# Putting the recurrence's 64x64 products on all four array tiles

## The chip, the cores and the metric

The kernel runs on one core of a Trainium2 chip. A core has a matrix engine (PE, which multiplies a moving operand by a stationary one and writes to the accumulation memory PSUM), three engines for element-wise work (DVE, ACT, POOL) and a queue engine (SP), which mostly issues transfers here. Memory on the core has 128 partitions; PSUM has eight banks. The metric is the device time of one execution in microseconds, the median of several runs. Lower is better.

The PE array is 128 rows by 128 columns. A product with 64 rows of stationary operand and 64 columns of output uses one of four tiles: rows 0-63 or 64-127 (the partitions on which the operands lie) by columns 0-63 or 64-127 (the partitions of PSUM to which the result goes). "Straight" tiles write to the partitions that they read from, "crossed" tiles write to the other half.

## The reference

One layer of a hybrid decoder for a prompt of 256 positions and 8 single-position decode sequences, width 2048: a gated feed-forward network of width 5504, then a mixing stage (an input projection, windowed attention with 16 query heads, and a linear recurrence with 16 heads of 64x64 state), an output projection, a second feed-forward network, and a final normalisation. All in float32. The part that matters is the recurrence, per head:

```
sa = S @ (-kk_t)
S  = S * exp(lw_t)[None, :] + outer(sa, kk_t * a_t) + outer(v_t, k_t)
y_t = S @ r_t
```

## The kernel before, in words

The kernel keeps activations transposed: features on partitions, 256 + 8 = 264 positions along the free dimension. Weights stream from memory in 128x512 chunks (`chunk`, L121): SP loads one, ACT rounds it to a "hi" part (L128), DVE makes the rest "lo" (L59 through L129), and PE does three products of 264 moving columns for each 128x128 block (`gemm`, L132). These weight products are named acc<-s,hi and the like in the profile. There are 1288 chunks and four hi and four lo buffers.

In the mixing stage the heads come in eight pairs, the two heads of a pair on the two halves of the partitions, and the pairs in four batches of two. The prompt's 256 positions are cut into four chunks of 64. For each pair `prep` (L415) makes the factors of the chunk form: Gm (products of keys and values of positions, masked), BT, KR and UV, and the products `gv` (L517) and, for the decode sequences, `dps` (L523). For each batch `chain` (L542) inverts a triangular matrix for each head and chunk (X, Y, TT on DVE, then the 32x32 products at L584 and L595), and then does the following, all with 64x64 blocks:

- W/U (L608): one product with 128 moving columns gives W and U of a head and chunk, the two heads on the two straight tiles. W goes to the tile `W` (L611), U to the free half of the tile `uv` (L615).
- P/G (L623, L626): W times BT gives P, copied to `PT` (L629); W times a part of Gm is added to KR (L630).
- N and Y (L637, L643): products with 128 rows and 64 columns over `uv`.
- three steps (L649 to L666), one for each later chunk: P times the state S (into `ps`), S times KR added to Y (into `pY`), and two DVE operations per pair that give the next S.
- Y is copied out of PSUM (L668), normalised (`gnorm`, L696) and gated.

`prep` and `chain` are generators: at a `yield` they hand over to the next weight product group, so that small products stand between weight products in PE's order. The order within each engine's queue is not that of the source: a scheduler orders the instructions of the whole program by a timeline of its own, with priorities. Each engine then runs its queue strictly in that order. The output projection's first part waits for batches 0 and 1 (L919), its second for batches 2 and 3.

PSUM banks for small products are taken by `mp` (L118) from a ring of five; weight products use a ring of three (L115). A bank is 128 partitions by 512 float32.

## Time and profile before

| | us |
|---|---|
| time, median of 3 runs | 1982.49 (1981.63 to 1985.6) |
| span of the profiled execution, first to last instruction | 1978.1 |
| PE busy | 1962.6 |
| DVE busy | 1318.0 |
| ACT busy | 1037.1 |
| POOL busy | 267.2 |

The profiled execution has only its span recorded; a time of its own is not among the listed runs, which lie 3.5 to 7.5 us above that span. The mixing stage lies between about 780 and 1160 us, the small products of `chain` between about 885 and 1090 us. In the profile a 32-bit product appears as two records (two passes), and "busy" counts the whole latency of overlapping records, so the pace of a stage is read from the start of one group to the start of the next. A released wait is shown in square brackets behind an instruction.

### The profile page before, as it was taken

The numbers are of one execution on the slowest core, as the hardware profiler recorded it, in microseconds if no ns is written. First come the engines' busy times: TensorE is split into PE (matmuls) and PEld (weight loads), VectorE is DVE, ScalarE is ACT, GpSimd is POOL, SyncE is SP. The second block draws the span as 40 slices with busy tenths as digits, with TensorE's granted clock in tenths as the row PEclk, the third lists the DMA queues.
The fourth block names the chain that finished last, engine by engine and source line by source line (L and its number), as shares of the span: only waits on it lengthen the run. The fifth ranks groups of instructions, "written<-read, shape, count | busy, mean of one in ns | idle before, by whom it ended". The sixth has DMA issues, their size and how long they took to land.

```text
span 1978.1 us, 45244 instructions
## 1 busy us (share of the span) xinstructions
PE 1962.6 (99%) x17011; PEld 1944.7 (98%) x17011; DVE 1318.0 (67%) x2591; ACT 1037.1 (52%) x2069; POOL 267.2 (14%) x382
## 2 busy tenths in 40 slices
PE   9999999999999999999999999999999999999998
PEld 9999999999999999999999999999999999999998
DVE  5865555655556567799988766866666666666655
ACT  5644444444444456666656754654444444444445
POOL 0401001010010113222211000210101001010012
PEclk9999999999999999999999999999999999999999
DMA  7565565655555567554545455565666566666654
GB/s 238 178 191 191 184 191 193 183 185 174 188 180 182 182 189 230 162 165 147 147 140 172 134 161 180 177 182 187 189 185 194 182 192 188 190 192 181 192 179 147
DMA packets 218875, 357.26 MB, mean 181 GB/s; under 512 B 33552, under 2 KB 72352, under 8 KB 218656
## 3 DMA queue, kind: packets, MB, share of 16 engines
q1 hardware_dynamic: 212144, 345.76, 56.1%
q10 hardware_dynamic: 6512, 8.61, 1.3%
q8 instruction: 133, 2.18, 0.4%
q14 instruction: 86, 0.70, 0.1%
HBM read 346.67 MB, written 9.69 MB: 180 GB/s over the span
## 4 chain that ended last, share of the span: by engine, by line
PE 96%; DVE 2%; DMA 1%; issue 1%; ACT 1%; SPq 0%; DVEq 0%; ACTq 0%
PE acc L75 88%; PE m L75 8%; DVE lo L59 0%; ACT t L69 0%; DMA x<-in_x 0%; DMA raw<-in_wout 0%; DVE y L59 0%; DVE st L59 0%; DVE Xt L59 0%; DMA sa<-gm 0%; DMA ld<-in_sT 0%; ACT hi L128 0%; PE m L505 0%; DVE t L705 0%; DVE gm L59 0%
## 5 line engine op out<-in xcount | busy, mean ns | idle before, releaser
L59 DVE TENSOR_TENSOR lo<-raw,hi 128x512 fp32r<-128x512 f32 (+1 forms) x1288 | 869.6, 679 | 526.9 <-ACT hi L128 504.5
L128 ACT CAST hi<-raw 128x512 fp32r<-128x512 f32 (+1 forms) x1288 | 777.4, 607 | 839.5 <-PE acc L75 766.0
L75 PE MATMUL acc<-s,hi 128*128 128x264 f32 x5940 | 1110.9, 286 | 2.3 <-DVE o L62 1.0
L75 PEld LDWEIGHTS acc<-s,hi 128*128 128x128 f32 x5940 | 923.4, 188 | 6.7 <-ACT hi L128 1.8
L75 PE MATMUL acc<-s,lo 128*128 128x264 f32 x2970 | 847.5, 286 | 0.5 <-DVE lo L59 0.5
L75 PEld LDWEIGHTS acc<-s,lo 128*128 128x128 f32 x2970 | 558.7, 188 | 2.2 <-DVE lo L59 0.9
L75 PE MATMUL acc<-t,hi 128*128 128x264 f32 x2752 | 502.8, 284 | 0.0
L75 PEld LDWEIGHTS acc<-t,hi 128*128 128x128 f32 x2752 | 426.0, 188 | 0.0
L75 PE MATMUL acc<-t,lo 128*128 128x264 f32 x1376 | 388.5, 284 | 0.0
L59 POOL TENSOR_TENSOR t<-t,t 128x264 f32<-128x264 f32 (+1 forms) x148 | 151.0, 1020 | 1146.6 <-ACT hi L128 789.4
L75 PEld LDWEIGHTS acc<-t,lo 128*128 128x128 f32 x1376 | 258.1, 188 | 0.0
L75 PE MATMUL acc<-y,hi 128*128 128x264 f32 x648 | 123.7, 284 | 0.0
L75 PEld LDWEIGHTS acc<-y,hi 128*128 128x128 f32 x648 | 101.2, 188 | 0.1
L75 PE MATMUL acc<-y,lo 128*128 128x264 f32 x324 | 91.9, 284 | 0.0
L59 DVE TENSOR_TENSOR t<-acc,t 128x264 f32<-128x264 f32 x156 | 67.4, 432 | 35.8 <-PE acc L75 35.5
L59 POOL TENSOR_TENSOR o<-o,o 128x264 f32<-128x264 f32 x43 | 35.8, 833 | 235.8 <-ACT o L69 231.8
L75 PE MATMUL acc<-o,hi 128*128 128x264 f32 x324 | 62.4, 282 | 0.0
L75 PEld LDWEIGHTS acc<-y,lo 128*128 128x128 f32 x324 | 60.8, 188 | 0.0
L69 ACT ACTIVATE t<-t 128x264 f32<-128x264 f32 (+1 forms) x110 | 46.6, 424 | 8.8 <-DVE t L433 5.5
L62 DVE SCALAR_TENSOR_TENSOR s<-acc,s 128x264 f32<-128x264 f32 x96 | 40.6, 427 | 15.5 <-PE acc L75 15.1
L75 PEld LDWEIGHTS acc<-o,hi 128*128 128x128 f32 x324 | 49.9, 188 | 0.0
L75 PE MATMUL m<-s,hi 128*128 128x264 f32 x260 | 47.9, 284 | 0.0
(261 smaller groups left out, 1283.5 us busy)
## 6 DMA issues: line engine op xcount, KB each, us to landing
raw<-in_gu SPq DMA_DIRECT2D x688, 256.0 KB, 3.3
raw<-in_dn SPq DMA_DIRECT2D x224, 256.0 KB, 2.8
raw<-in_win SPq DMA_DIRECT2D x152, 256.0 KB, 3.4
raw<-in_dn SPq DMA_DIRECT2D x160, 192.0 KB, 2.7
raw<-in_wout SPq DMA_DIRECT2D x64, 256.0 KB, 3.2
xsp<-x ACTq DMA_DIRECT2D x16, 132.0 KB, 3.4
s<-xsp SPq DMA_DIRECT2D x16, 132.0 KB, 4.0
ld<-in_sT SPq DMA_DIRECT2D x16, 128.0 KB, 2.9
```

The lines of the kernel that those rows point to most:

```text
L59: return e.tensor_tensor(out=out, in0=a, in1=b, op=op)
L62: return V.scalar_tensor_tensor(out=out, in0=a, scalar=s, in1=b, op0=op0, op1=op1)
L69: return A.activation(out=out, in_=in_, func=f, **k)
L75: return TE.matmul(out, lhsT, rhs, start=start, stop=stop, **k)
L128: A.copy(hi[:, :w], raw[:, :w])
```

## The change

Products that used only the two straight tiles are distributed over four:

- W and U are separate products of 64 columns. U goes to the crossed tiles, so head h's U lies in PSUM on the other half's partitions, and W stays on the straight tiles. W of chunk 0, which nobody reads, is no longer computed. U and W have a bank each for both pairs of the batch, instead of one bank per pair. The copies into `uv` read from the other half, one for each half instead of one for each half and pair.
- P goes to the crossed tiles and G to the straight ones, in a bank each; the copies into `PT` swap the halves.
- In the three steps the products for `ps` stay straight, those for `pY` go crossed, and the two kinds alternate. The first products for `pY` also write to the other half. The copy out of `pY` is split in halves, one on ACT and one on DVE.
- In `prep` the products for `gv` (crossed already) and `dps` (straight already) alternate instead of following one another, with both banks taken at the start.

```diff
-                gv = mp()
-                for c in range(4):
+                gv, dps = mp(), mp()
+                for i in range(NB):
+                    c, g = i // 2, i % 2
                     for h in range(2):
                         r, o = HALF[h], HALF[1 - h]
-                        mm(gv[r, c * 64:c * 64 + 64], bt.Gm[k][h][o, c, 0:64], bt.UV[o, c, k, r])
+                        mm(dps[r, 2 * i:2 * i + 2], st[i // 4][r, i % 4, :], XD[r, 6:8, p, i])
+                        if h == g:
+                            mm(gv[r, c * 64:c * 64 + 64], bt.Gm[k][h][o, c, 0:64], bt.UV[o, c, k, r])
                 A.copy(KR[:, 2], gv[:, :256].rearrange("p (c t) -> p c t", c=4))
-                dps = mp()
-                for i in range(NB):
-                    for h in range(2):
-                        r = HALF[h]
-                        mm(dps[r, 2 * i:2 * i + 2], st[i // 4][r, i % 4, :], XD[r, 6:8, p, i])
...
-                wus = [mp() for _ in range(n)]
+                ub, wb = mp(), mp()
                 for k in range(n):
                     for c in range(4):
+                        x = (k * 4 + c) * 64
                         for h in range(2):
-                            r = HALF[h]
-                            mm(wus[k][r, c * P:c * P + P], TT[r, k * 4 + c, :], bt.KR[k][r, 0:3:2, c, :])
+                            r, o = HALF[h], HALF[1 - h]
+                            mm(ub[o, x:x + 64], TT[r, k * 4 + c, :], bt.KR[k][r, 2, c, :])
+                            if c:
+                                mm(wb[r, x:x + 64], TT[r, k * 4 + c, :], bt.KR[k][r, 0, c, :])
+                v = wb[:, :n * 256].rearrange("p (k c t) -> p k c t", k=n, c=4)
                 for k in range(n):
-                    v = wus[k].rearrange("p (c t) -> p c t", c=4)
-                    (A.copy, V.tensor_copy)[k % 2](W[:, k], v[:, 1:4, 0:64])
-                for k in range(n):
-                    v = wus[k].rearrange("p (c t) -> p c t", c=4)
-                    for h in range(2):
-                        (V.tensor_copy, A.copy)[h](uv[HALF[h], :, k, HALF[h]], v[HALF[h], :, 64:128])
+                    (A.copy, V.tensor_copy)[k % 2](W[:, k], v[:, k, 1:4, :])
+                v = ub[:, :n * 256].rearrange("p (k c t) -> p c k t", k=n, c=4)
+                for h in range(2):
+                    (V.tensor_copy, A.copy)[h](uv[HALF[h], :, :, HALF[h]], v[HALF[1 - h]])
                 yield
-                pbs = [mp() for _ in range(n)]
+                pb, gb = mp(), mp()
                 for k in range(n):
                     for c in range(1, 4):
...
-                            mm(pbs[k][r, x:x + 64], W[r, k, c - 1, :], bt.BT[k][r, c, r])
...
-                            mm(pbs[k][r, x + 64:x + P], W[r, k, c - 1, :], bt.Gm[k][h][r, c, 64:128])
+                            mm(pb[o, x:x + 64], W[r, k, c - 1, :], bt.BT[k][r, c, r])
+                            mm(gb[r, x:x + 64], W[r, k, c - 1, :], bt.Gm[k][h][r, c, 64:128])
+                v = pb[:, :n * 192].rearrange("p (k c t) -> p k c t", k=n, c=3)
+                for h in range(2):
+                    A.copy(PT[HALF[h]], v[HALF[1 - h]])
...
-                            mm(pY[r, x:x + 64], uv[:, c, k, r], bt.Gm[k][h][:, c, 64:128],
+                            mm(pY[HALF[1 - h], x:x + 64], uv[:, c, k, HALF[h]], bt.Gm[k][h][:, c, 64:128],
                                k + c == 0, c == 0, skip_group_check=True)
...
                         for h in range(2):
-                            r = HALF[h]
+                            r, o = HALF[h], HALF[1 - h]
                             mm(ps[r, k * 64:k * 64 + 64], PT[r, k, c - 1, :], S[r, k])
-                    for k in range(n):
-                        for h in range(2):
-                            r = HALF[h]
-                            x = (k * 4 + c) * 64
-                            mm(pY[r, x:x + 64], S[r, k], bt.KR[k][r, 1, c, :], False, True, skip_group_check=True)
+                            mm(pY[o, x:x + 64], S[r, k], bt.KR[k][r, 1, c, :], False, True, skip_group_check=True)
...
                 for k in range(n):
-                    A.copy(Ys[k][:, :NP], pY[:, k * NP:(k + 1) * NP])
+                    for h in range(2):
+                        (A.copy, V.tensor_copy)[h](Ys[k][HALF[h], :NP], pY[HALF[1 - h], k * NP:(k + 1) * NP])
```

More of the change, by code (lines that the diff above doesn't have):

```diff
@@ L627, in chain @@
+                v = pb[:, :n * 192].rearrange("p (k c t) -> p k c t", k=n, c=3)
+                for h in range(2):
+                    A.copy(PT[HALF[h]], v[HALF[1 - h]])
+                v = gb[:, :n * 192].rearrange("p (k c t) -> p k c t", k=n, c=3)
                 for k in range(n):
-                    v = pbs[k][:, :384].rearrange("p (c t) -> p c t", c=3)
-                    A.copy(PT[:, k], v[:, :, 0:64])
-                    tt(V, bt.KR[k][:, 1, 1:4, :], v[:, :, 64:128], bt.KR[k][:, 1, 1:4, :], ALU.add)
+                    tt(V, bt.KR[k][:, 1, 1:4, :], v[:, k], bt.KR[k][:, 1, 1:4, :], ALU.add)
@@ L651, in chain @@
                     for k in range(n):
+                        x = (k * 4 + c) * 64
                         for h in range(2):
[L653 removed]
+                            r, o = HALF[h], HALF[1 - h]
                             mm(ps[r, k * 64:k * 64 + 64], PT[r, k, c - 1, :], S[r, k])
[L655 to L659 removed]
+                            mm(pY[o, x:x + 64], S[r, k], bt.KR[k][r, 1, c, :], False, True, skip_group_check=True)
                     Z, Sn = ring((P, n, 64), "Z", 2), ring((P, n, 64), "S", 3)
```

6 lines of the change are left out of this document (1 added, 5 removed).

## The prediction

> **What bounds the kernel now.** I read the page first (busy shares, chain), then the timeline of PE around the recurrence, then ACT's and DVE's at the same places, and last the order in which the changed program lists its instructions.
>
> ```profile
> PE 1962.6 (99%) x17011; PEld 1944.7 (98%) x17011; DVE 1318.0 (67%) x2591; ACT 1037.1 (52%) x2069; POOL 267.2 (14%) x382
> ...
> PE 96%; DVE 2%; DMA 1%; issue 1%; ACT 1%; SPq 0%; DVEq 0%; ACTq 0%
> ```
>
> PE is busy all the time and owns 96% of the chain. So a microsecond of PE's stream removed is worth a microsecond, as long as PE is not sent to wait for something instead. "Busy" overlaps, so I take prices from start to start. One batch of two head pairs, first batch:
>
> ```profile
> 895.82 1.96 PE L75 MATMUL m<-kr,TT 64*64 64x128 f32 x32
> 897.71 0.39 PE L75 MATMUL acc<-s,hi 128*128 128x264 f32 x1
> ...
> 899.36 0.33 PE L75 MATMUL m<-BT,W 64*64 64x64 f32 x4
> ...
> 900.91 1.15 PE L75 MATMUL m<-uv,BT 128*64 128x64 f32 x32
> ...
> 907.86 0.45 PE L75 MATMUL m<-S,PT 64*64 64x64 f32 x8
> ...
> 908.47 0.39 PE L75 MATMUL acc<-s,lo 128*128 128x264 f32 x1
> ```
>
> The columns are start, length, engine, line, operation, tiles and count. A 64x64 product leaves two records (two passes). The W/U products (L608) take 897.71 - 895.82 = 1.89 us for 32 records, the P/G products (L623, L626) 900.91 - 899.36 = 1.55 us for 48, and one step of the recurrence (L654, L659) 908.47 - 907.86 = 0.61 us for 16. The next fence is the prep of both pairs (L517 and L523), where products on the crossed tiles (uv,gm) already meet products on the straight ones (XD,ld):
>
> ```profile
> 833.34 0.51 PE L75 MATMUL m<-uv,gm 64*64 64x64 f32 x10
> 833.64 0.22 PE L75 MATMUL m<-XD,ld 64*64 64x2 f32 x2
> 833.68 0.23 PE L75 MATMUL m<-uv,gm 64*64 64x64 f32 x2
> 833.72 0.20 PE L75 MATMUL m<-XD,ld 64*64 64x2 f32 x2
> 833.74 0.22 PE L75 MATMUL m<-uv,gm 64*64 64x64 f32 x2
> 833.77 0.20 PE L75 MATMUL m<-XD,ld 64*64 64x2 f32 x2
> 833.80 0.23 PE L75 MATMUL m<-uv,gm 64*64 64x64 f32 x2
> 833.83 0.72 PE L75 MATMUL m<-XD,ld 64*64 64x2 f32 x20
> ...
> 835.69 0.39 PE L75 MATMUL acc<-s,hi 128*128 128x264 f32 x1
> ```
>
> This fence decides most. A pair of crossed records starts every 0.06 us (833.68, 833.74, 833.80), and between them a pair of straight records, also every 0.06 us (833.72, 833.77, 833.83). So a tile takes one record in about 0.058 us, also for 2 moving columns, and four tiles do run at once: four records in 0.058 us where the other stages do two. 48 records on two tiles make 24 x 0.058 = 1.40 us, and 1.55 measured leaves 0.15 for changing the tile size. With 128 moving columns the slot is (1.89 - 0.15)/16 = 0.109 us.
>
> **The change part by part.**
>
> W/U: 32 records of 128 columns become 56 of 64 (64 calls of U, 48 of W over all batches, two records each, since chunk 0's W is dropped). U's 32 lie on the two crossed tiles and set the time: 16 x 0.058 + 0.15 = 1.08 us, a gain of 0.81. P/G: 24 records on each pair of tiles, 12 x 0.058 + 0.15 = 0.85, gain 0.70. A step: 4 x 0.058 + 0.15 = 0.38, gain 0.23, three steps. Prep: 835.69 - 833.34 = 2.35 now; the 64 records of the straight tiles remain, 32 x 0.058 + 0.15 = 2.01, gain 0.34. The Y products (L643) only change halves: nothing. Four batches: 4 x (0.81 + 0.70 + 0.69 + 0.34) = 10.2 us less on PE.
>
> Bounds: if crossed and straight tiles did not overlap, 56 records at 0.029 would take 1.62 instead of 1.74, a gain of 0.5 in all, and the rest nothing. Four moving streams of 64 columns at once are not in the trace; four records per slot were seen for three slots only. The fastest long run is 32 records of 32x32 tiles in 0.63 us (1068.30 to 1068.93, below), 0.020 each; at that pace the gain falls by 4 x (0.19 + 0.26 + 0.28) = 2.9 to 7.3. I take 9.5, close to the overlapped row, which is the same tile size.
>
> The Trainium skill (TensorE: Matmul & The Clock Gate, "Part 3: Packing small matmuls") says a weight load overlaps a running matmul only where the row group differs, which would forbid the straight and the crossed tile of one half to run together. By it the gain would be the 0.5 above. The 833 rows show the opposite, both tiles of a half served in one slot.
>
> Copies:
>
> ```profile
> L615 ACT COPY uv<-m 64x256 f32<-64x256 f32 x8 | 2.9, 368 | 2.4 <-DVE uv L615 2.2
> ...
> L629 ACT COPY PT<-m 128x192 f32<-128x192 f32 x8 | 2.4, 319 | 0.9 <-PE m L75 0.8
> ```
>
> 64 more columns cost about 0.05 us. U: two copies of 512 columns (0.57 each) for four of 256, 0.17 less on ACT and about as much on DVE. P: two of 64x384 (0.47) for two of 128x192, 0.3 more on ACT. Y: the two copies of 128x256 become four half-height ones, two of them on DVE, 0.8 more there. All lie beside weight products: in the changed order 22 such products (0.12 us each) stand between W/U and P/G where 12 stood, and 22 to 26 between steps. I cost them at nothing; with the cover gone they would cost 0.3 to 0.8 per batch, up to 3.
>
> Now the order. In the changed program the last batch is packed differently. Today 25 weight products stand between the 32x32 products (TT,W, L594) and W/U, and the products of w_out begin after all of Y. In the changed order two W/U calls follow TT,W directly, with nothing between, and w_out's first products stand between W/U and P/G. The rows of today's last batch, PE then ACT:
>
> ```profile
> 1064.84 0.92 PE L75 MATMUL m<-s,o 128*128 128x256 f32 x4
> 1065.51 0.37 PE L75 MATMUL acc<-s,hi 128*128 128x264 f32 x1
> ...
> 1068.30 0.69 PE L75 MATMUL m<-TT,W 32*32 32x32 f32 x32
> 1068.93 0.39 PE L75 MATMUL acc<-s,hi 128*128 128x264 f32 x1
> ...
> 1072.18 1.96 PE L75 MATMUL m<-kr,TT 64*64 64x128 f32 x32
> ```
>
> ```profile
> 1064.95 0.74 ACT L589 COPY W<-m 32x256 f32<-32x256 f32 x2 [1.35 <-PE m L75]
> 1065.92 0.62 ACT L128 CAST hi<-raw 128x512 fp32r<-128x512 f32 x1 [0.23 <-PE acc L75]
> 1066.56 1.28 ACT L69 ACT_TABLE_LOAD   x1
> ...
> 1069.63 0.47 ACT L69 ACTIVATE stc<-sta,vec 128x2 f32<-128x2 f32 x2
> 1070.00 0.60 ACT L128 CAST hi<-raw 128x512 fp32r<-128x512 f32 x1
> 1070.62 0.75 ACT L598 COPY TT<-m 32x256 f32<-32x256 f32 x2
> ```
>
> W/U needs the TT copies. In the changed order they keep their place on ACT: W copies, one cast, table load, four exponentials, stc, TT copies (one cast less). From the PE products ahead of the W copies to the end of the TT copies that is 0.11 + 0.74 + (1070.00 - 1065.92) + 0.75 = 5.7 us. PE then has 7 weight products (0.85), four score products (2 x 0.6) and TT,W (0.63): 2.7 us. So PE waits about 3.1 us, or up to 4.9 if the score maxima, which stand later on DVE there, hold the exponentials; I take 3.9. Then w_out's first products need casts of the mixed heads, and P/G its W copy. Prices on ACT:
>
> ```profile
> 1075.60 0.80 ACT L69 ACTIVATE t<-t,stb 128x256 f32<-128x256 f32 x2
> 1076.30 0.63 ACT L774 COPY t<-m 128x256 f32<-128x256 f32 x2
> ...
> 1079.87 1.04 ACT L910 CAST s<-y 128x264 fp32r<-128x264 f32 x3
> ```
>
> Ahead of that W copy stand four exponentials (1069.63 - 1066.56 - 1.28 = 1.8) with stc (0.4), two pairs of scalings (0.7 each), two PSUM copies (0.6) and five casts (0.35 each): with W itself and the ways between engines 6.4 us. PE's cover is W/U 1.1, six transposes 0.6, 20 weight products 2.4: 2.3 us waited. Today's PE waits in this stage include
>
> ```profile
> PE acc L75 <- DVE o L62: 1.0, 1, 1.0
> PE m L75 <- DVE uv L615: 0.7, 1, 0.7
> ```
>
> of which the second lies inside the last batch's P/G, for DVE's half of W; it falls together with the wait just priced and goes. New waits: 3.9 + 2.3 - 0.7 = 5.5, between 0 (if ACT gets there early) and 7.
>
> The clock drops today just behind this place:
>
> ```profile
> 1088.00:1090.00 2.00, 2.00 (x23) 1.45 (x22) 0.89 (x4) 1.07 (x4) 0.24 (x1) 0.71 0.81 230
> 1090.00:1092.00 2.00, 2.00 (x14) 1.88 (x12) 0.77 (x3) 1.39 (x5) 0.00 (x0) 0.50 0.55 175
> 1092.00:1094.00 2.00, 2.00 (x17) 2.00 (x17) 1.23 (x3) 0.64 (x2) 0.00 (x0) 0.94 0.08 16
> ```
>
> The columns are busy time of PE, its weight loads, DVE, ACT and POOL, then granted clock. The clock is 0.50 with PE "busy", after a stretch of tiny products. 0.29, 0.50 and 0.06 of three times 2 us are missing: 1.7 us of full speed lost. An empty stretch may bring a second such drop: between 0 and 1.7, I take 0.6. The Trainium skill (TensorE: Matmul & The Clock Gate, "Part 1: The HAM clock gate") puts the drop behind an idle window of about 3.4 us; the trace shows that it also comes without idleness.
>
> DVE is full in parts of this stage, and each microsecond that PE gains brings its demand forward:
>
> ```profile
> 990.00:1010.00 20.00, 18.96 (x149) 18.07 (x149) 19.76 (x48) 12.27 (x26) 5.08 (x11) 1.00 0.50 153
> ```
>
> PE idles 1.0 us here already. For small waits of that kind I add 0.5 (0 to 9, see the rival).
>
> Sum: -9.5 + 5.5 + 0.6 + 0.5 = -2.9 us against the profiled span of 1978.1, so 1975.2 in span. The runs' median of 1982.49 stands 4.4 above the span; I carry that over: 1979.6.
>
> **The rivals.** (1) The waits of the last batch do not appear, because ACT reaches the TT copies early or other work fills in: -10.2 to -8 with some loss, about 1974. For it: PE has 99% today; against it: ACT cannot begin the 5.7 us before PE's own products. (2) Slower: DVE sets the pace of batches 0 to 2. 19.76 of 20 us is full; with two more Y copies and less in U it has 0.6 more per batch. If it is the bound from 930 to 1010, the PE gain of three batches (7.1) is void and 3 x 0.6 comes on top: 1988. It decides from the point where DVE has no idle time left in a batch, some 2.5 us in 67. Against it: PE itself waits for DVE only 1.0 us there. (3) The change does not do what it says: the four tiles do not overlap with full streams. Gain 0.5, waits 4.5 (the longer W/U fills some), clock and small waits 1.1: +5, 1987.5. Against it the 833 rows.
>
> **How the numbers follow.** My forecast has 0.42 (its own range 1976 to 1983.5), rival 1 0.27, rival 2 0.13, rival 3 0.12, and 0.06 is left for orders that I misread. 0.2% is 4 us, about what runs of this kernel can tell from no change (1981.63 to 1985.6). A third of the forecast's share and all of rival 1 lie below 1978.5: 0.41. Rivals 2 and 3 lie mostly above 1986.5, with some of the rest: 0.21. The remainder, 0.38, is no change. The range goes from the whole gain without waits (1972) to rival 2 (1988).
>
> **What would show it.** Four-tile stages: kr,TT should span 1.1 us instead of 1.89, P/G 0.85 instead of 1.55, a step 0.38 instead of 0.61; if they keep today's spans, rival 3 holds. PE should show one wait of 3 to 5 us on ACT's TT copies and shorter ones on the s and W copies in the last batch; without them rival 1. Longer PE waits on DVE between 930 and 1010 would be rival 2. The prediction is wrong if the four-tile pace is off by a third, or if the last batch's waits are far from 5.5.

## The result, and the profile after

The changed kernel takes 1985.01 us (median of 12 executions, 1983.45 to 1989.61) against 1983.36 for the kernel before (12 executions, 1978.27 to 1985.6). The ratio on record is 1.0020, 95% interval 1.0013 to 1.0027: by this ratio about 4 us slower, where 2.9 us faster was predicted. The two medians alone lie only 1.65 us apart; beside the experiments below the kernel before took medians of 1980.77 to 1981.93, 3 to 4 us under 1985.01. So the sign is clear, the size is somewhere from 1.7 to 4 us. The profiled execution has a span of 1982.1 us (its own time is 1983.9), against 1978.1 before. In every execution on record with both numbers the time is about 1.8 us above the span, so the profiled execution of before took about 1979.9 us: it is one of the faster ones of its kernel, and of the 4.4 us that the prediction carried from its span to the median only 1.8 belong to every execution.

The page of the changed kernel, busy shares and chain:

```profile
PE 1958.9 (99%) x17107; PEld 1939.7 (98%) x17107; DVE 1320.4 (67%) x2595; ACT 1040.3 (52%) x2067; POOL 264.4 (13%) x382
...
PE 94%; DVE 3%; ACT 1%; DMA 1%; issue 1%; SPq 0%; POOL 0%; DVEq 0%; ACTq 0%
```

PE is busy for 3.7 us less and the span is 4.0 us longer; DVE has gone from 2% to 3% of the chain and PE from 96% to 94%. So the shorter products are there, and waits and lost clock have taken more than they gave. First the products, in PE's timeline of the first batch (start, length, engine, line, operation, tiles, count):

```profile
895.14 1.15 PE L75 MATMUL m<-kr,TT 64*64 64x64 f32 x56
896.23 0.39 PE L75 MATMUL acc<-s,hi 128*128 128x264 f32 x1
...
899.10 0.27 PE L75 MATMUL m<-BT,W 64*64 64x64 f32 x1
...
899.27 0.22 PE L75 MATMUL m<-BT,W 64*64 64x64 f32 x1
899.27 0.22 PE L75 MATMUL m<-gm,W 64*64 64x64 f32 x1
899.28 0.22 PE L75 MATMUL m<-BT,W 64*64 64x64 f32 x1
899.29 0.22 PE L75 MATMUL m<-gm,W 64*64 64x64 f32 x1
899.33 0.22 PE L75 MATMUL m<-BT,W 64*64 64x64 f32 x1
...
899.96 1.15 PE L75 MATMUL m<-uv,BT 128*64 128x64 f32 x32
...
907.05 0.27 PE L75 MATMUL m<-S,PT 64*64 64x64 f32 x1
...
907.44 0.51 PE L75 MATMUL acc<-s,hi 128*128 128x264 f32 x2
```

Four records, two straight (gm) and two crossed (BT), start within 0.02 us, and the next four 0.058 us later. W/U takes 1.09 us, P/G 0.86, a step 0.39: the prediction's 1.08, 0.85 and 0.38.

Then the waits of PE from 780 to 1160 us (engine, tile and line, releaser and its line, us in total, times, longest):

```profile
PE m L75 <- ACT TT L596: 5.3, 2, 2.9
PE acc L75 <- DVE o L62: 1.5, 2, 1.0
PE m L75 <- DVE PT L59: 1.5, 1, 1.5
PE m L75 <- DVE Xt L59: 1.4, 1, 1.4
PE m L75 <- DVE W L612: 1.0, 1, 1.0
PE m L75 <- DVE st L59: 0.9, 1, 0.9
```

With two more of 0.7 us together these make 12.3 us; the same view of the kernel before makes 5.3. By place: in the last batch (1060 to 1110 us) the waits go from 1.7 to 2.9 us; between 920 and 1060 us, where the second and third batch's products run on PE, from 1.9 to 7.9. (The batches are counted from one here; the fourth is the last. While one batch's products run on PE, the next batch's substitution, the steps that invert its triangles, runs on DVE: the third's from about 960 us, the fourth's from about 1030.) The prediction looked for the loss in the last batch, and most of it is ahead of it.

What stands behind the waits between 920 and 1060 is on DVE. Its timeline in the changed kernel:

```profile
956.65 0.42 DVE L59 TENSOR_TENSOR kr<-t,t 128x256 f32<-128x256 f32 x1
960.23 0.19 DVE L59 TENSOR_TENSOR st<-X,Xt 128x30 f32<-128x30 f32 x1 [3.16 <-DMA Xt<-sa]
...
961.75 0.43 DVE L59 TENSOR_TENSOR pj<-acc,rs 128x264 f32<-128x264 f32 x1
...
1027.05 0.17 DVE L59 TENSOR_TENSOR t<-m,t 128x8 f32<-128x8 f32 x1 [4.00 <-POOL t L59]
...
1030.46 0.19 DVE L59 TENSOR_TENSOR st<-X,Xt 128x30 f32<-128x30 f32 x1 [2.59 <-DMA Xt<-sa]
```

DVE's timeline in the kernel before, the same two places:

```profile
959.95 1.29 DVE L59 TENSOR_TENSOR lo<-raw,hi 128x512 fp32r<-128x512 f32 x2 [0.94 <-ACT hi L128]
961.16 0.18 DVE L59 TENSOR_TENSOR st<-X,Xt 128x30 f32<-128x30 f32 x1
...
1019.97 0.17 DVE L59 TENSOR_TENSOR t<-m,t 128x8 f32<-128x8 f32 x1 [4.55 <-POOL t L59]
...
1024.48 0.19 DVE L59 TENSOR_TENSOR st<-X,Xt 128x30 f32<-128x30 f32 x1 [2.75 <-DMA Xt<-sa]
```

`st<-X,Xt 128x30` is the first instruction of a batch's substitution (L562). It needs the triangles, which `prep` writes to memory (sa) and which SP loads again as X and Xt. Before, in the third batch, DVE had two more weight chunks (`lo`) to do directly ahead of it, and the load had landed when it came to the substitution (961.16, no wait); after, the first product stands ahead of those chunks and DVE, which works in order, stands still for 3.16 us until Xt lands. What stands behind it in DVE's order waits as long: `lo` chunks, `pj`, and the W copies and `o` that PE needs.

In the fourth batch the stall is no longer than before (2.59 us, 2.75 before). Ahead of it DVE also stands 4.00 us for a small product of POOL (`t<-m,t`), and this too is in both kernels (4.55 before). New in the changed kernel are thus the third batch's stall, and that PE waits behind the fourth's (0.98 us at 1040.81 and 0.89 at 1045.83; nothing there before).

The SP queue of the changed kernel shows when the loads of the third batch are issued:

```profile
953.35 0.53 SPq L551 DMA_DIRECT2D Xt<-sa  x1
...
954.58 1.91 SPq L551 DMA_DIRECT2D Xt<-sa  x3
```

The last piece of Xt is issued by 956.5 and DVE goes on at 960.23.

One way from DVE's stall to PE goes over ACT. ACT's timeline, the changed kernel and then the kernel before:

```profile
962.95 0.35 ACTq L873 DMA_DIRECT2D out_sh<-shc  x1
963.39 0.62 ACT L128 CAST hi<-raw 128x512 fp32r<-128x512 f32 x1 [4.71 <-POOL shc L401]
964.03 0.75 ACT L596 COPY TT<-m 32x256 f32<-32x256 f32 x2
```

```profile
960.46 0.75 ACT L598 COPY TT<-m 32x256 f32<-32x256 f32 x2
...
964.79 0.34 ACTq L876 DMA_DIRECT2D out_sh<-shc  x1
```

And PE's rows in the changed kernel (start, length, what, idle time before it and its releaser):

```profile
964.45 1.57 PE L75 MATMUL m<-kr,TT 64*64 64x64 f32 x56 [2.45 <-ACT TT L596]
...
976.12 0.24 PE L75 MATMUL m<-N,PT 64*64 64x64 f32 x1 [1.37 <-DVE Xt L59]
...
1040.81 0.27 PE L75 MATMUL m<-BT,W 64*64 64x64 f32 x1 [0.98 <-DVE W L612]
...
1077.85 0.33 PE L75 MATMUL m<-kr,TT 64*64 64x64 f32 x4 [2.90 <-ACT TT L596]
```

`pj` (DVE 961.75, behind the stall) is the last product that POOL needs for shc (L401); the store of shc is issued from ACT's queue; ACT stands 4.71 us at that issue, and the TT copies queue behind it. In the kernel before this store stands behind the TT copies.

A ledger makes this comparable over all kernels. Between two weight products that every kernel has (the 6000th and the 10500th, about 767 to 1480 us) every start-to-start interval on PE is counted as work, as a wait (over 0.36 us, outside half-clock stretches), or, where the trace's clock record says 0.5, half as work and half as lost clock. Before: 704.8 work, 6.9 waits, 1.7 clock. After: 695.8, 16.0 and 5.0, that is **-9.0, +9.1, +3.3**, together +3.4 us. (16.0 is more than the 12.3 of the waits because an interval runs from start to start and so holds the product ahead of the wait too, 0.2 to 0.3 us each time.) It is one execution for each kernel, and not always a typical one: e5's profiled execution took 1979.05 us against a median of 1983.65, e10's 1983.97 against 1982.08, e7's 1981.29 against 1979.30. The clock term above all differs between executions, and the eight kernels with the whole change, whose products are the same, have work terms from -8.8 to -10.8.

### The profile page after: what moved, and what is told of

The parts are those of the page before. It is cut to its first block, busy times and chain, and to the rows that moved or that the text cites. A ratio compares the mean times of both kernels' runs of the same rounds, so it can differ in the third digit from the quotient of the medians.

```text
span 1982.1 us, 45417 instructions
## 1 busy us (share of the span) xinstructions
PE 1958.9 (99%) x17107; PEld 1939.7 (98%) x17107; DVE 1320.4 (67%) x2595; ACT 1040.3 (52%) x2067; POOL 264.4 (13%) x382
## 4 chain that ended last, share of the span: by engine, by line
PE 94%; DVE 3%; ACT 1%; DMA 1%; issue 1%; SPq 0%; POOL 0%; DVEq 0%; ACTq 0%
PE acc L75 87%; PE m L75 7%; DVE lo L59 1%; ACT t L69 0%; DVE st L59 0%; DVE Xt L59 0%; DMA x<-in_x 0%; DVE y L59 0%; DMA s<-xsp 0%; SPq L551 0%; DMA Xt<-sa 0%; ACT hi L128 0%; DVE y L62 0%; PE m L505 0%; DMA ld<-in_bias 0%
```

## The experiments

In the expectations, Q is the theory that ACT's queue (the stores issued from it) makes the waits, D that the place of the next batch's substitution on DVE makes them, and W that the W/U part is slow for a reason of its own. P and C stand for a full DVE ("pace") and for missing weight products between the last batch's small ones ("cover"). Where nothing else is said a kernel starts from the changed one. The kernel before ran anew beside each group, and the ratios are to these executions (medians 1980.77 us for e1 to e4, 1981.28 for e5 to e8, 1981.70 for e9 to e11, 1981.93 for e12 and e13, 1981.04 for e14 to e16). All results; the last three columns are the ledger's differences to the profiled execution of before, in us:

| kernel | median, us | ratio to before (95%) | work | waits | clock |
|---|---|---|---|---|---|
| the change | 1985.01 | 1.0020 (1.0013 to 1.0027) | -9.0 | +9.1 | +3.3 |
| e1 sh store late | 1988.56 | 1.0031 (1.0018 to 1.0043) | -8.8 | +10.5 | +5.0 |
| e2 sh, kp, vp stores late | 1989.23 | 1.0038 (1.0026 to 1.0051) | -10.5 | +12.8 | +7.1 |
| e3 the same in before | 1981.71 | 1.0003 (0.9994 to 1.0011) | -0.3 | +2.8 | +1.7 |
| e4 W/U part alone | 1986.42 | 1.0025 (1.0016 to 1.0033) | -4.1 | +8.6 | 0.0 |
| e5 substitution behind the uv copy | 1983.65 | 1.0004 (0.9995 to 1.0013) | -9.7 | +7.6 | +0.8 |
| e6 the same in before | 1981.78 | 1.0003 (0.9994 to 1.0012) | -0.8 | +2.9 | 0.0 |
| e7 third substitution two turns later | 1979.30 | 0.9991 (0.9982 to 1.0000) | -10.6 | +9.5 | +2.7 |
| e8 before, two turns earlier | 1994.47 | 1.0059 (1.0046 to 1.0071) | -1.3 | +8.4 | +8.2 |
| e9 all parts but W/U | 1978.59 | 0.9983 (0.9974 to 0.9991) | -6.4 | +1.8 | +5.1 |
| e10 P/G part alone | 1982.08 | 1.0005 (0.9996 to 1.0014) | -3.0 | +5.8 | +1.6 |
| e11 steps alone | 1980.57 | 0.9991 (0.9982 to 1.0000) | -3.8 | +0.7 | +3.5 |
| e12 W/U alone, one turn later | 1986.12 | 1.0022 (1.0013 to 1.0030) | -3.4 | +5.5 | +1.6 |
| e13 e9, one turn earlier | 1983.29 | 1.0007 (0.9998 to 1.0016) | -6.5 | +6.1 | +1.7 |
| e14 substitution behind first W/U product | 1979.57 | 0.9989 (0.9980 to 0.9998) | -10.4 | +5.2 | +6.7 |
| e15 e14 with stores late | 1979.34 | 0.9991 (0.9982 to 0.9999) | -10.8 | +6.8 | +3.3 |
| e16 e14's edit in before | 1984.54 | 1.0014 (1.0005 to 1.0023) | +1.1 | +2.0 | +1.7 |

**e1 to e3: is it ACT's queue?** e1 issues the store of shc late, behind a weight product group, so that ACT does not stand there; e2 also moves the stores of kp and vp, and e3 does e2's moves in the kernel before.

```diff
-                    if len(bat) == len(BATCH):
-                        A.dma_start(O["sh"], shc)
...
+                    if i == 3:
+                        behind(A.dma_start(O["sh"], shc))
```

```diff
-                    A.dma_start(O[("kp", "vp")[w]][p, r], xs[h % len(xs)][r, P:NP])
...
                 yield
+                for h in range(2):
+                    behind(A.dma_start(O[("kp", "vp")[w]][p, HALF[h]], xs[h % len(xs)][HALF[h], P:NP]))
```

> The changed kernel, with one DMA issue moved: the store of the shift state (out_sh) leaves ACT's queue ahead of the TT copies of the second batch and is put behind the key and value tiles. Nothing else moves on PE. Theory Q (a queue): the 2.4 us in which PE waits for TT in the second batch is ACT standing in front of this DMA; PE's wait on TT falls from 5.3 to 2.9 us (only the last batch's is left), and the half-clock stretch behind it (some 1.5 us lost) goes because that 3.4 us window is no longer empty: 1985.0 - 2.4 - 1.5 = 1981.1, 0.999 of the kernel before. Rival P (pace): in batches 0 to 2 DVE is the bound and the queue only shows it; then PE waits for DVE elsewhere in the second batch for as long, and the time stays at 1985.

> As the run before, and the key and value stores (out_kp, out_vp) go behind the PT copies in ACT's queue too. By this the order of the last batch changes as well: 29 weight products stand between TT,W and W/U where none stood. Theory Q: the 1.5 us wait ahead of the first step of the second batch (PT copies behind the out_kp issues) goes, and with the cover back the last batch's wait on TT (2.9) falls under 0.5 us and its half-clock stretch (1.4) goes: 1981.1 - 1.5 - 2.6 - 1.4 = 1975.6, 0.996 of the kernel before. Rival P (pace): 1985, with the waits moved to DVE. Rival C (the last batch's chain on ACT is simply long): the TT wait moves to the W copy ahead of P/G: 1979.

> The same moves of the stores' issue in the kernel before. Theory Q: there the issues stood behind the TT and PT copies already, so nothing waits less: 1983.4 within 1.5 us, ratio 0.9995 to 1.0005. If the moves are worth something by themselves, whatever the products do, this run gains as much as the second one does over the changed kernel.

In e1 the wait on TT at the third substitution's stall is gone (2.45 us in the changed kernel), and PE waits for the W copies behind it instead. PE's timeline of e1, and ACT's ahead of it:

```profile
971.41 0.27 PE L75 MATMUL m<-BT,W 64*64 64x64 f32 x1 [2.40 <-ACT W L612]
973.28 0.27 PE L75 MATMUL m<-BT,W 64*64 64x64 f32 x1 [1.29 <-DVE W L612]
```

```profile
970.40 0.61 ACT L69 ACTIVATE t<-t,less,half 128x264 f32<-128x264 f32 x1 [5.66 <-DVE t L62]
```

ACT's half of W (971.04) stands behind this row, which waits 5.66 us for a product of DVE: without the store, ACT is late for DVE directly.

DVE's of e2, and then PE's of e2 behind it:

```profile
1031.11 0.19 DVE L59 TENSOR_TENSOR st<-X,Xt 128x30 f32<-128x30 f32 x1 [5.03 <-DMA Xt<-sa]
```

```profile
1009.28 0.52 PE L75 MATMUL acc<-s,hi 128*128 128x264 f32 x2 [4.07 <-DVE o L62]
...
1042.58 0.36 PE L75 MATMUL m<-BT,W 64*64 64x64 f32 x1 [6.09 <-DVE W L612]
```

In e2 the last batch's wait on TT is gone as well (29 weight products stand between the TT,W products and W/U there, none in the changed kernel), and the kernel is 0.38% slower than before: DVE's stall in the fourth batch grew to 5.03 us, and PE then waits 6.09 us for DVE's half of W. In e3 DVE stands 4.84 us there, PE waits only 2.03 for W, and the time is that of the kernel before. So the queue of ACT is one way along which the stall reaches PE, and taking the store out of the way gains nothing: Q falls as the cause of the loss. The slow ones of these kernels share two stalls on Xt, in the third and in the fourth batch; e3 has the fourth's alone.

**e4, e9, e10, e11: which part of the change?** e4 has the W/U part alone in the kernel before; e9 is the change without it; e10 has the P/G part alone, e11 the steps (with the Y products and copies) alone. The core of the edit in e4 (from before), and of e9 (from after):

```diff
-                wus = [mp() for _ in range(n)]
+                ub, wb = mp(), mp()
...
-                            mm(wus[k][r, c * P:c * P + P], TT[r, k * 4 + c, :], bt.KR[k][r, 0:3:2, c, :])
+                            mm(ub[o, x:x + 64], TT[r, k * 4 + c, :], bt.KR[k][r, 2, c, :])
+                            if c:
+                                mm(wb[r, x:x + 64], TT[r, k * 4 + c, :], bt.KR[k][r, 0, c, :])
```

```diff
-                ub, wb = mp(), mp()
+                wus = [mp() for _ in range(n)]
...
-                            mm(ub[o, x:x + 64], TT[r, k * 4 + c, :], bt.KR[k][r, 2, c, :])
-                            if c:
-                                mm(wb[r, x:x + 64], TT[r, k * 4 + c, :], bt.KR[k][r, 0, c, :])
+                            mm(wus[k][r, c * P:c * P + P], TT[r, k * 4 + c, :], bt.KR[k][r, 0:3:2, c, :])
```

of e10 and of e11 (both from before):

```diff
-                            mm(pbs[k][r, x:x + 64], W[r, k, c - 1, :], bt.BT[k][r, c, r])
...
-                            mm(pbs[k][r, x + 64:x + P], W[r, k, c - 1, :], bt.Gm[k][h][r, c, 64:128])
+                            mm(pb[o, x:x + 64], W[r, k, c - 1, :], bt.BT[k][r, c, r])
+                            mm(gb[r, x:x + 64], W[r, k, c - 1, :], bt.Gm[k][h][r, c, 64:128])
```

```diff
-                            mm(pY[r, x:x + 64], S[r, k], bt.KR[k][r, 1, c, :], False, True, skip_group_check=True)
+                            mm(pY[o, x:x + 64], S[r, k], bt.KR[k][r, 1, c, :], False, True, skip_group_check=True)
...
-                    A.copy(Ys[k][:, :NP], pY[:, k * NP:(k + 1) * NP])
+                    for h in range(2):
+                        (A.copy, V.tensor_copy)[h](Ys[k][HALF[h], :NP], pY[HALF[1 - h], k * NP:(k + 1) * NP])
```

> One part of the change alone, on the kernel before: U on the crossed tiles and W on the straight ones; prep, P/G and steps as before. PE's gain 4 x 0.81 = 3.2 us. In this order the out_sh issue stands ahead of the TT copies of the second batch too, and 25 weight products stay between TT,W and W/U in the last batch. Theory Q: one wait on TT, of about 2 us, in the second batch and none in the last; 1983.4 - 3.2 + 2.4 + 0 to 1.5 of clock = 1982.6 to 1984.1. Rival P or C: no wait on TT, since the pace or the long last batch made it: 1980.2.

> The change without its W/U part (prep, P/G and steps on four tiles; W/U as in the kernel before). In this order the substitutions stand where they stand in the kernel before (5 and 2 weight chunks behind the gm products), the shift state's store stands behind the TT copies, and 28 weight products stay between TT,W and W/U in the last batch. PE's part falls by 2.8 (P/G) + 2.8 (steps) + 1.1 (prep) = 6.7 us. Theory D (the loss came with the substitution moved ahead of its load, which the W/U part does): no new wait, ratio to before 0.9965 to 0.998. Rival P (DVE sets the pace of batches 0 to 2, so that PE's gain is void there): 0.9995 to 1.001.

> P/G alone on four tiles, the rest as before; substitutions at 5 and 2 weight chunks. PE 2.8 us less. Theory D: ratio 0.9985 to 0.9995. Rival P: 0.9995 to 1.0005.

> The steps on four tiles with the crossed Y alone, the rest as before; substitutions at 5 and 2 weight chunks, 30 weight products between TT,W and W/U in the last batch. PE 2.8 us less. Theory D: ratio 0.9985 to 0.9995. Rival P: 0.9995 to 1.0005; the two Y copies that DVE gets (0.8 us a batch) would show as PE waits on DVE.

The W/U part alone loses 0.25%, and everything else without it gains 0.17% and beats both kernels. I counted the weight chunks that DVE does between the last Gm product of `prep` and the first `st`, in the third and fourth batch: 5 and 2 before, 5 and 2 with the P/G part, the steps or e9, 3 and 1 with the W/U part alone and with the whole change. So one part moves the substitution forward, and it is the part with the loss. e4's DVE stands 2.28 us in front of the third substitution (PE then waits 1.48 for TT, 0.40 for W, 0.80 for st) and 3.25 in front of the fourth. e9 waits for Xt too, in the fourth batch, and it hardly reaches PE. DVE's row of e9, and then PE's:

```profile
1027.10 0.19 DVE L59 TENSOR_TENSOR st<-X,Xt 128x30 f32<-128x30 f32 x1 [3.91 <-DMA Xt<-sa]
```

```profile
1038.40 0.24 PE L75 MATMUL m<-N,PT 64*64 64x64 f32 x1 [0.38 <-DVE st L59]
```

How much of a stall in front of the fourth substitution reaches PE differs between the kernels. Where the third substitution does not stall, the stall and PE's waits on W and st behind it are 2.75 and 0 in the kernel before, 3.43 and 0 in e11, 3.91 and 0.38 in e9, 4.11 and 2.20 in e12, 4.84 and 2.03 in e3, 5.50 and 3.19 in e10 (where the trace names another load that was issued behind Xt, ld, as the one that ended the stall): some 2 to 3.5 us are hidden. Where the third one stalls too, less is hidden or nothing: 2.59 and 1.87 in the changed kernel, 2.92 and 1.40 in e13, 3.25 and 1.46 in e4, 3.83 and 2.77 in e1, 5.06 and 5.52 in e8, 5.03 and 6.09 in e2; e7 with 5.16 and 2.46 is the exception. That the first stall has used up the slack for the second would explain it, but no run tests it. In e10's profiled execution the waits (+5.8) take more than P/G's shorter products give (-3.0). And DVE is not full around the stall. The stretch in e10 (busy time of PE, its weight loads, DVE, ACT, POOL, then granted clock):

```profile
1018.00:1036.00 18.00, 14.71 (x307) 13.74 (x305) 9.15 (x35) 9.22 (x25) 1.82 (x7) 1.00 0.51 143
```

DVE works 9.15 of 18 us: here it is late because it stands, not because it has too much to do.

**e5 to e8: hold the substitution, or bring it forward.** e5 places the first product of the third and fourth substitution behind the uv copy of the batch before, by a dependence in the order alone (nothing waits for it on the chip, but the scheduler orders the rest anew); e6 does this in the kernel before. e7 only lets the third batch's chain wait for 13 instead of 11 turns, e8 lets it wait for 9 in the kernel before.

```diff
+                after = None
+                if bt.i in (2, 3):
+                    while bts[bt.i - 1].wu is None:
+                        yield
+                    after = bts[bt.i - 1].wu
...
-                    keep = behind if s == 1 else lambda i: i
+                    keep = (lambda i: behind(i, after)) if s == 1 else lambda i: i
...
+                    x = (V.tensor_copy, A.copy)[h](uv[HALF[h], :, :, HALF[h]], v[HALF[1 - h]])
+                    if not h:
+                        bt.wu = x
```

```diff
-DWAIT = (11, 11, 11, 3)
+DWAIT = (11, 11, 13, 3)
```

```diff
-DWAIT = (11, 11, 11, 3)
+DWAIT = (11, 11, 9, 3)
```

> The changed kernel; the first product of the substitution (st from X and Xt) of the third and fourth batch is held on DVE behind the uv copy of the batch before. In the changed kernel it stands earlier (3 and 1 weight chunks behind the gm products instead of 5 and 2), and DVE stands 3.2 and 2.6 us in front of it until the load of Xt lands, with pj, W, uv, o behind it. With the hold 24 weight products also stand between TT,W and W/U in the last batch. Theory D (DVE stands in front of a load): DVE's wait on Xt falls from 5.7 to under 0.5 us; PE's waits in the second and third batch (2.45 on TT, 1.37, 0.98, 0.89) go; the last batch's wait on TT (2.9) falls under 0.5; the half-clock stretches behind the first and the last of these (1.5 and 1.4) go: 1985.0 - 5.7 - 2.6 - 2.9 = 1973.8, ratio 0.995. Rival P (DVE is full, and works off the same amount later): the waits come back at PT,gm and in the steps, 1985 to 1988.

> The same hold in the kernel before. DVE's 2.7 us in front of the load in the fourth batch go, and PE's 1.0 on o with them at most. But here the order packs the last batch as the changed kernel does: no weight product between TT,W and W/U. Theory C (cover): PE waits 2.5 to 3.5 us on TT there, with up to 1.5 us of half clock behind it; ratio to before 1.0005 to 1.002. If the wait belongs to the four tiles and not to the order, it does not come, and the ratio is 0.999 to 1.000.

> The changed kernel with two more ticks (13 for 11) ahead of the substitution of the third batch alone: 5 weight chunks behind the gm products, as in the kernel before. The last batch stays packed (nothing between TT,W and W/U, 3 weight products between W/U and P/G). Theory D: DVE's wait on Xt falls from 5.7 to 2.6; PE's 2.45 on TT and 1.37 ahead of the first step in the second batch go, and the half clock behind the first (1.5); the waits of the last batch stay, with 1 to 2 more on the W copy: 1985.0 - 5.3 + 1.5 = 1981, ratio 0.999. Rival P: 1985 or more, ratio 1.002.

> The kernel before with two ticks less (9 for 11) ahead of the substitution of the third batch: 3 weight chunks behind the gm products, as in the changed kernel; no product changes. Theory D: DVE stands some 3 us in front of the load while the second batch's W/U and P/G run, and PE waits 2 to 5 us on copies there: ratio to before 1.001 to 1.0025. Rival P: DVE has slack or is the bound anyway, ratio 1.000.

e8 is the strongest result: in the kernel before, with no product changed, an earlier third substitution costs 0.59%. The third batch's stall, the one that the edit moved, is only 1.49 us; the longest is that of the fourth batch, 5.06 us, with the fourth's place unchanged at 2 weight chunks. Of the 15.3 us that the ledger gives in its profiled execution, 8.4 are waits and 8.2 lost clock. DVE's row in the fourth batch, and then PE's:

```profile
1033.89 0.19 DVE L59 TENSOR_TENSOR st<-X,Xt 128x30 f32<-128x30 f32 x1 [5.06 <-DMA Xt<-sa]
```

```profile
1011.61 0.48 PE L75 MATMUL acc<-s,hi 128*128 128x264 f32 x2 [2.64 <-DVE o L62]
...
1040.63 0.48 PE L75 MATMUL m<-BT,W 64*64 64x64 f32 x4 [5.52 <-DVE W L611]
```

e7 goes the other way and turns the change from 0.20% slower into a kernel no slower than before (0.9991, the interval ends at 1.0000). But not as D has it: D expected DVE's wait on Xt to fall from 5.7 to 2.6 us, and in e7's profiled execution DVE stands 1.29 us in front of the third substitution (the trace names the store of shc as what ended this) and 5.16 in front of the fourth, 6.45 together. PE's waits are no fewer either (+9.5); they lie at other places, 4.04 us of them on ACT's s in the last batch. So the place of the substitution decides here, but the length of the stalls does not tell how. e5 removes every stall on Xt, where D expected a ratio of 0.995, and gets 1.0004: it is too late with the fourth substitution. PE's row of e5:

```profile
1070.01 1.06 PE L75 MATMUL m<-PT,gm 32*32 32x32 f32 x32 [6.13 <-DVE PT L59]
```

So both sides can cost: too early, and DVE stands for the load; too late, and the last batch waits for its inverse. e6 does not settle what cover the last batch has in the kernel before, because this wait on PT, 2.10 us there, moved ahead of the place.

**e12 and e13: the same lever on the parts.** e12 is e4 with DWAIT (11, 11, 12, 3), e13 is e9 with (11, 11, 10, 3).

```diff
-DWAIT = (11, 11, 11, 3)
+DWAIT = (11, 11, 12, 3)
```

```diff
-DWAIT = (11, 11, 11, 3)
+DWAIT = (11, 11, 10, 3)
```

> W/U alone on four tiles, as in the run of that part, with one tick more (12 for 11) ahead of the substitution of the third batch; it then stands 5 weight chunks behind the gm products (3 in that run) and the fourth batch's 2 (1 in that run), as in the kernel before. Theory D (the W/U part loses by where its order puts the substitution): the ratio to before falls from 1.0025 to between 0.998 and 1.0005; DVE's wait on Xt falls from 5.5 us to about 3. Rival W (the part loses by its own copies: one uv copy of 512 columns on each engine, 0.69 us on DVE, where two of 256 stood): it stays between 1.0015 and 1.003.

> All but the W/U part, as in the run that gave 0.9983, with one tick less (10 for 11) ahead of the substitution of the third batch: 3 weight chunks behind the gm products instead of 5. The products are the same. Theory D: DVE stands 2 to 4 us in front of the load while the second batch's W/U and P/G run, and the ratio to before rises to between 1.0005 and 1.004. Rival W: the place does not matter, 0.998 to 0.999.

e13 came out at the time that D says: the fastest kernel loses 0.24% when its third substitution starts one turn earlier. DVE then stands 1.34 us in front of the third and 2.92 in front of the fourth, and PE waits 0.92, 0.70, 0.59 and 1.16 us for W copies; but e9 had 3.91 us in front of the fourth alone, so it is where DVE stands, and not for how long, that has changed. e12 did not: 1.0022 against e4's 1.0025, no recovery. PE's waits of e12 from 780 to 1160 us:

```profile
PE m L75 <- ACT W L614: 2.5, 1, 2.5
...
PE m L75 <- DVE W L614: 1.5, 1, 1.5
```

The waits at the third substitution fell, from 1.48, 0.40 and 0.80 us to 0.57. But the fourth batch's stall rose from 3.25 to 4.11 us (1.5 and 0.7 waited on W and st; 1.5 on W in e4), and the last batch's wait for ACT's W from 1.6 to 2.5. That D holds for the W/U part alone is therefore not shown by this kernel, and W is not excluded by it.

**e14 to e16: hold at the earliest point where the load should be there.** e14 places the two substitutions behind the first W/U product of the batch before, in the scheduler's order only, which lets them start 3.2 and 1.2 us earlier than in e5; e15 adds e2's late stores; e16 is e14's edit in the kernel before, as a control. Beside e5's first two hunks:

```diff
-                            mm(ub[o, x:x + 64], TT[r, k * 4 + c, :], bt.KR[k][r, 2, c, :])
+                            i = mm(ub[o, x:x + 64], TT[r, k * 4 + c, :], bt.KR[k][r, 2, c, :])
+                            bt.wu = bt.wu or i
```

> The whole change, the substitution of the third and fourth batch ordered behind the first W/U product of the batch before: 6 and 3 weight chunks behind the gm products (3 and 1 in the changed kernel, 5 and 2 in the kernel before; the hold behind the uv copy gave 7 and 6). 16 weight products ahead of TT,W and 11 within W/U in the last batch. Theory D: DVE's wait on Xt falls from 5.7 to 1 to 3 us, the waits in the second and third batch (5.7 in all) fall under 2, and no wait like the 6.1 us on PT of the run with the later hold: ratio to before 0.995 to 0.998. Rival W (the W/U part loses by its own copies wherever the substitution stands): 0.9995 to 1.002.

> The same hold, with the stores of shift state, keys and values behind the TT and PT copies on ACT; 6 and 3 weight chunks. Theory D: as the run beside it, 0.995 to 0.998; in the run with the stores moved alone PE waited behind DVE's two stalls (3.4 and 5.0 us), and those are gone here. Rival W: 0.9995 to 1.002.

> The same hold in the kernel before: 5 and 3 weight chunks (5 and 2 without). DVE's stall in the fourth batch falls from 2.7 to 1 to 2 us; PE's wait behind it was 1.0. Ratio to before 0.9985 to 1.0005, so that what the hold gains in the changed kernel is not a gain of the hold by itself.

With the whole change kept, products and copies alike, the loss of 0.20% turns into a gain of 0.11% (D expected 0.2 to 0.5%, so most of the shorter products' 0.5% is still lost). DVE does 6 and 3 weight chunks ahead of the two substitutions and does not wait for Xt; one of the new waits of the last batch is then the one that the prediction priced at 2.3 us. PE's rows of e14:

```profile
973.68 0.24 PE L75 MATMUL m<-N,PT 64*64 64x64 f32 x1 [1.11 <-DVE Xt L59]
...
1077.48 0.91 PE L75 MATMUL m<-BT,W 64*64 64x64 f32 x12 [2.50 <-ACT W L619]
```

The control says that the hold is no gain by itself: in the kernel before it loses 0.14%. So e14's 0.31% over the changed kernel, taken between their ratios to before, comes from taking back a shift that the change had made, not from a better place for both kernels. e15 is no different from e14. And with the W/U part e14 has 4 us less work than e9 and is no faster (0.9989, 0.9983): what W/U's shorter products give is lost even with this hold.

Three kernels beat both the kernel before and the changed one, by ratios whose intervals exclude 1: e9 (0.9983), e14 (0.9989) and e15 (0.9991); the last two by little, out of sixteen kernels tried.

## Why the prediction was wrong

**PE's shorter products: right.** Predicted -9.5, measured -9.0 in the profiled execution. In the first batch, before to after: W/U 1.89 to 1.09 us (0.81 predicted, 0.80 found), P/G 1.55 to 0.86 (0.70, 0.69), a step 0.61 to 0.39 (0.23, 0.22), the first prep 2.35 to 2.04 (0.34, 0.31). The row that decided, four records in one slot of 0.058 us, was read rightly from three slots. Rival 3 falls, and with it the reading of the Trainium skill's rule (TensorE: Matmul & The Clock Gate, "Part 3: Packing small matmuls") that would have forbidden the straight and the crossed tile of one half to run together.

**Copies at nothing: no trace of a loss from their lengths.** What matters about them is when they start.

**The last batch: half right.** The wait on ACT's TT copies was predicted at 3.9 and measured at 2.90 us, inside the 3 to 5 us only by rounding. The prediction's own sum for it, 5.7 - 2.7, is 3.0 (it wrote 3.1) and was right; the 0.9 that it put on top for late score maxima did not come. And the wait on W, 2.3 predicted, did not come in the changed kernel (in e14 it is 2.50, in e12 2.53). The term was +5.5; the waits from 1060 to 1110 us rose by 1.2.

**The step that failed: "For small waits of that kind I add 0.5 (0 to 9, see the rival)."** Outside the last batch PE's waits with a named releaser rose by 5.8 us (by 7.0 in all, 1.2 of them in the last batch), and the rise is between 920 and 1060 us. The range held it, the value was 0.5. In all, 6.0 us of waits were predicted and 9.1 measured in the ledger, most of them in another place; and of the 6.3 us between the predicted -2.9 and the ledger's +3.4, the waits make 3.1, the clock 2.7 and the products 0.5. The prediction looked for new waits in the changed order of the last batch alone. On DVE the order shows, without any run, that the third and fourth substitution move from 5 and 2 weight chunks behind the triangles' last products to 3 and 1; and the kernel before has the warning in its fourth batch, where DVE stands 2.75 us on the same load (1024.48) without PE waiting behind it.

**Rival 2 came nearer to the number (1988), by another mechanism.** That is luck in part: rival 3's 1987.5 is as near, and its mechanism is refuted. Rival 2 has longer waits of PE on DVE between 930 and 1010; there are 1.9 us of them, 1.0 before. It has DVE full, and in parts DVE is. Two stretches of the changed kernel (columns as above):

```profile
950.00:970.00 20.00, 17.50 (x277) 16.15 (x272) 15.53 (x50) 10.75 (x30) 4.25 (x15) 0.91 0.59 163
...
990.00:1010.00 20.00, 19.51 (x147) 18.63 (x146) 19.66 (x45) 14.02 (x29) 1.78 (x7) 1.00 0.44 138
```

From 990 to 1010 DVE works 19.66 of 20 us, 19.76 before; from 950 to 970 it works 15.53, against 17.96 before, because it stands for Xt. So DVE has not too much work, but once it is late it has little room to catch up before 1010. The two readings differ in what to do: a full DVE needs work taken away, a standing one needs another order, and e14 and e7, which take no work away, win the loss back.

**The clock: +0.6 (0 to 1.7) predicted, +3.3 measured in the profiled execution.** Three half-clock stretches with 1.7 us lost in each, instead of one: the first and the last come behind the two waits for TT copies, the second behind the last batch's prep, where PE starts nothing but small products. The term allowed one more.

What is shown: that an earlier third substitution alone slows a kernel (e8, e13), that a later one alone speeds the changed kernel (e7, e14), that the W/U part is the one that moves it forward (the counts of e4, e9, e10, e11), and that DVE then stands in front of it for Xt (the rows). What is argued only: that the stalls on Xt are the way by which the place costs time. For it speak the changed kernel's rows from stall to wait; against it, that e7 is faster than the changed kernel with longer stalls, and that D's forecasts of the ratio missed in e5, e10, e12, e14, e15 and narrowly e9 (slower than expected), e16 (slower than expected for the control) and e8 (over twice the loss expected). What stays open: why e12 did not recover, so whether the W/U part has a cost beside this one; and why the scheduler moves the substitution. That its timeline has the loads landing sooner than they do is only a guess from the order that it makes.

## What to carry to other kernels

Where a scheduler orders the whole program, a change that shortens one engine's stage reorders the others; compare the order of every engine over every batch, and look first at what stands ahead of an instruction that waits for a transfer on an engine working in order. A stall in front of such an instruction can cost nothing in one kernel (2.75 us in the fourth batch before) and be felt in the next (2.59 us at the same place, and 1.87 waited behind it), so a wait that is harmless in the old profile is a place where a faster neighbour can show up as a loss. Try the same hold in the old kernel as well: only then is it known whether it repairs the change or improves both.

## What the runs showed of the hardware

**Half-clock stretches sit on a grid.** In the changed kernel's clock record the three stretches at 0.5 inside the mixing stage are 3.413 us long each (in e2, e5, e7, e8 and e14 some are 6.827, two lengths); they start at 965.81, 1027.25 and 1078.45 us, 61.44 and 51.20 us apart, which is 18 and 15 times 3.413. Where one of the eighteen traces has several stretches between 50 and 1900 us, they lie whole multiples of 3.413 us apart. The changed kernel in windows of 2 us (columns as above):

```profile
962.00:964.00 2.00, 0.00 (x0) 0.00 (x0) 1.36 (x6) 0.61 (x1) 0.68 (x1) 1.00 0.51 139
...
966.00:968.00 2.00, 2.00 (x10) 2.00 (x10) 2.00 (x7) 0.00 (x0) 0.00 (x0) 0.50 0.55 130
```

PE starts nothing from 962 to 964, works through W/U, and then runs its weight products at half speed (0.220 us start to start instead of 0.121). So here a wait of 2.45 us cost up to 1.7 us more, half of one stretch. The Trainium skill (TensorE: Matmul & The Clock Gate, "Part 1: The HAM clock gate") has a free-running window of 3413 ns, which the length and the grid bear out, and a drop after an idle window; here PE started W/U 1.4 us ahead of the first drop, so if the windows are the cells of this grid, one with part of it idle was enough. Every one of the 46 stretches from 50 to 1900 us in the eighteen traces follows a grid cell in which at most 11 weight products start (28 fill one). But most such cells bring no drop: the grid cells at 1085.3 (after) and 1146.9 (before), in which no weight product starts, have none behind them; why is open.

**Equal executions differ by the clock.** In e9's twelve executions the span goes with the mean granted clock, from 1974.1 us at 0.998 to 1979.7 at 0.994: 5.6 us, more than the whole effect of the change. A difference of 0.2% needs many executions of both kernels, and the ledger's clock term for one execution is only an example.
